# Retention keys and outputs transposed on TensorE into a free PSUM bank, in place of 32x32 block transposes on VectorE

## The chip, the cores and the metric

The kernel runs on one core of one Trainium2 chip. A core has a matrix engine (TensorE, PE in the rows; PEld is its weight load), three elementwise engines (VectorE, DVE; ScalarE, ACT; GpSimd, POOL), a queue that issues transfers (SyncE, SP), an on-chip memory SBUF, and eight accumulator banks of 128 partitions by 512 float32 called PSUM, into which the matrix engine writes. The metric is the device time of one execution in microseconds (us). Each engine works through its own queue in order, and waits where an instruction needs a result of another engine.

## The reference, cut to what matters

Two transformer blocks run one after the other on 1024 tokens of width 1024. The change lies in the second block, in its retention branch with 4 heads, key and value width 256:

```
qb = rotary(split_heads(r_q, 4));  kb = rotary(split_heads(r_k, 4)) * 256 ** -0.5
scores = (q k^T) * gamma^|t-s|  inside a chunk;  intra = scores @ v
step:  out   = (q * q_decay) @ state
       state = state * chunk_decay + (k * k_decay)^T @ v
ret = rms_norm(intra + inter, ret_out_gain);  out_b = merge_heads(ret) * silu(r_g)
```

The state update needs the keys with tokens on the partitions, while the scores need them with features there. The output is normalised with tokens on the partitions and is needed afterwards with features there. So keys and outputs are transposed once each.

## The kernel before

Activations are kept as two float32r parts (a rounded one and the rest), and each product of matrices is three matmuls into one accumulator (`PASSES`). The second block computes stick-breaking attention, then retention, then the merge of both branches. Retention takes the time from about 1440 to 2042 us of the profiled span.

For each head `h` in turn `ret_proj` (L1091) computes the projections: queries and keys with features on the partitions (`dense_col`, L112, copied to `ro` by ACT on L1098), rotated by DVE (L1103 to L1106) and POOL (L1107, L1108); values with tokens on the partitions (`dense_tok`, L102, split into `v` by ACT on L1116 and DVE on L1117); the gate (L1121). The weights are brought in by SP and split by POOL (L70, L71) into `wu`.

`ret_chain` (L1141) then works in two groups `g` of four 128-token tiles `j`. For a group it computes scores (L1151 into `psc`, shown as `pz`), masks and splits them (L1153 to L1157), transposes the keys of the group on DVE with `dve_transpose` (L128) into `kf`, and makes the decayed keys `kd` from `kf`: the rounded part on ACT (L1162), the rest on DVE (L1163). For a tile it computes the output `po` (L1171, L1179; shown as `pt`, in bank "t"), the sum of squares on ACT (L1184), the inverse root on POOL (L125, L126, tile `ss`), the scaled output `ot` on DVE (L1186), and the state update (L1192 into `pst`, shown as `po`, L1196 or L1198, split on L1202 and L1203). After four tiles the group's output is transposed by `dve_transpose` into `ob`, scaled by ACT (L1209), gated by POOL (L1210) and stored by SP (L1212). `kf` and `ob` use one buffer, tag "ob".

`dve_transpose` is 16 instructions, one for each pair of 32-partition blocks:

```
for a in range(4):
    for b in range(4):
        nc.vector.transpose(out=dst[32 * b:32 * b + 32, :, :, 32 * a:32 * a + 32],
                            in_=src[32 * a:32 * a + 32, :, :, 32 * b:32 * b + 32])
```

PSUM is split by tags: three banks "a" for the large products, two "z", and one each of "p", "t" and "o". Retention leaves "p" unused. The order of instructions on each engine is not written out by hand: the framework's scheduler places them by its own estimate of times, and mixes the chain of one head with the projections of the next, and the last chain with the merge products (`merge_logits`, L951). In heads 1 and 2 `attention_gates` (L1125) is mixed in, whose ACT instruction (L1134) waits for a load.

Of the kernel before, what the change touches and what calls it, by code (L numbers as in the profile page):

```python
# [11 lines left out]
F32 = mybir.dt.float32  # L12
F32R = mybir.dt.float32r
AF = mybir.ActivationFunctionType
ALU = mybir.AluOpType
# [4 lines left out]
P = 128  # L20
# [7 lines left out]
def f32(ap):  # L28
    return ap.bitcast(F32)
# [7 lines left out]
def tile_kernel(ctx: ExitStack, tc: tile.TileContext, I: dict, out: bass.AP, dbg=None, stop=None):  # L37
    nc = tc.nc
# [13 lines left out]
    ident = const.tile([P, P], F32, name="ident")  # L52
# [71 lines left out]
    def rsqrt_small(dst, src, mul, eps, eshape):  # L124
        nc.gpsimd.tensor_scalar(out=dst, in0=src, scalar1=mul, scalar2=eps, op0=ALU.mult, op1=ALU.add)  # L125
        nc.gpsimd.tensor_tensor(out=dst, in0=dst, in1=mhalf[:, :eshape], op=ALU.pow)  # L126

    def dve_transpose(dst, src):  # L128

        for a in range(4):  # L130
            for b in range(4):
                nc.vector.transpose(out=dst[32 * b:32 * b + 32, :, :, 32 * a:32 * a + 32],  # L132
                                    in_=src[32 * a:32 * a + 32, :, :, 32 * b:32 * b + 32])

# [944 lines left out]
    with tc.tile_pool(name="rt", bufs=1) as rt:  # L1079
# [61 lines left out]
        def ret_chain(h, tiles):  # L1141
            qTs, kTs, vs = tiles
            state = None
            for g in range(2):
# [3 lines left out]
                for j in range(4):  # L1148
                    cs = slice(j * P, (j + 1) * P)
                    for b in range(2):  # L1150
# [7 lines left out]
                kd = [rt.tile([P, 4, 256], F32R, tag="kd%d" % x, name="kd") for x in range(2)]  # L1158
                kf = rt.tile([P, 4, 256], F32, tag="ob", name="kf")
                dve_transpose(kf.rearrange("p n (b c) -> p b n c", b=2), kT.rearrange("p b (n c) -> p b n c", n=4))  # L1160
                kf, kh, kl = [t_.rearrange("p a b -> p (a b)") for t_ in [kf] + kd]
                nc.scalar.activation(out=kh, in_=kf, func=AF.Copy, scale=rdv[:, h, 0:1])  # L1162
                nc.vector.scalar_tensor_tensor(out=kl, in0=kf, scalar=rdv[:, h, 0:1], in1=f32(kh),  # L1163
                                               op0=ALU.mult, op1=ALU.subtract)
                ot = rt.tile([P, 4, 256], F32, tag="ot", name="ot")
# [38 lines left out]
                ob = rt.tile([P, 2, 4, P], F32, tag="ob", name="ob")  # L1204
                dve_transpose(ob, ot.rearrange("p n (b c) -> p b n c", b=2))
                for b in range(2):
                    ga = rt.tile([P, 512], F32, tag="ga", name="gb", bufs=2)
                    nc.sync.dma_start(out=ga, in_=d_gb[2 * h + b, :, g * 512:(g + 1) * 512])
                    nc.scalar.activation(out=ob[:, b], in_=ob[:, b], func=AF.Copy, scale=rgn[:, 2 * h + b:2 * h + b + 1])  # L1209
                    nc.gpsimd.tensor_tensor(out=ob[:, b].rearrange("p n c -> p (n c)"), in0=ob[:, b].rearrange("p n c -> p (n c)"),  # L1210
# [137 lines left out]
```

## Time and profile before

| | |
|---|---|
| median of 3 runs | 2317.09 us (2314.77 to 2318.42) |
| profiled execution, whole time | 2316.85 us |
| its span on the core | 2315.1 us |
| PE busy | 2182.2 us (94%) |
| DVE busy | 1242.6 us (54%) |
| ACT busy | 879.1 us (38%) |
| POOL busy | 1210.2 us (52%) |

The span reaches from the first instruction to the end of the last; the whole time has 1.75 us more around it. Busy times of engines overlap each other. For PE the busy time holds overlapping matmuls, so the time from the start of one matmul to the start of the next is what a matmul takes of the engine, and the idle time in front of a matmul is what a wait costs.

### The profile page before, as it was taken

The numbers are of one execution on the slowest core, as the hardware profiler recorded it, in microseconds if no ns is written. First come the engines' busy times: TensorE is split into PE (matmuls) and PEld (weight loads), VectorE is DVE, ScalarE is ACT, GpSimd is POOL, SyncE is SP. The second block draws the span as 40 slices with busy tenths as digits, with TensorE's granted clock in tenths as the row PEclk, the third lists the DMA queues.
The fourth block names the chain that finished last, engine by engine and source line by source line (L and its number), as shares of the span: only waits on it lengthen the run. The fifth ranks groups of instructions, "written<-read, shape, count | busy, mean of one in ns | idle before, by whom it ended". The sixth has DMA issues, their size and how long they took to land.

```text
span 2315.1 us, 33643 instructions
## 1 busy us (share of the span) xinstructions
PE 2182.2 (94%) x12197; PEld 1875.5 (81%) x12197; DVE 1242.6 (54%) x2228; ACT 879.1 (38%) x2191; POOL 1210.2 (52%) x1435
## 2 busy tenths in 40 slices
PE   7998888899999988999999999999989999999999
PEld 7777877787898778988888888788878788788887
DVE  4688789844457555665566453327474744321221
ACT  5344434445544225565566544012222222321200
POOL 6667778762004345554565545536575754434531
PEclk9999999999999999999999999999999999999999
DMA  4266830054486431110111103221324333644433
GB/s 129 83 165 166 206 86 26 35 159 130 146 280 215 147 106 42 55 47 23 51 51 55 51 32 97 67 69 55 125 87 132 95 105 101 218 164 152 142 106 107
DMA packets 238791, 249.25 MB, mean 108 GB/s; under 512 B 40032, under 2 KB 173856, under 8 KB 238368
## 3 DMA queue, kind: packets, MB, share of 16 engines
q1 hardware_dynamic: 238624, 247.10, 34.0%
q8 instruction: 96, 1.57, 0.3%
q14 instruction: 71, 0.58, 0.1%
HBM read 171.51 MB, written 75.53 MB: 107 GB/s over the span
## 4 chain that ended last, share of the span: by engine, by line
PE 43%; POOL 7%; DVE 7%; issue 4%; DMA 3%; ACT 3%; SPq 0%; POOLq 0%; ACTq 0%
PE acc L112 26%; PE acc L102 9%; PE acc L859 3%; POOL wu L71 2%; DMA raw<-in_w_in_dram 2%; PE po L1063 2%; DVE A L1042 1%; POOL wu L70 1%; DVE A L1037 1%; POOL A L1047 1%; PE pt L1179 1%; POOL ss L126 1%; ACT A L1036 1%; DVE xo L909 1%; DVE kf L132 1%
## 5 line engine op out<-in xcount | busy, mean ns | idle before, releaser
L112 PE MATMUL acc<-h2h,wu 128*128 128x512 f32 x1504 | 460.5, 396 | 0.7 <-POOL wu L71 0.4
L102 PE MATMUL acc<-wu,h2h 128*128 128x384 f32 (+1 forms) x1536 | 374.5, 326 | 11.5 <-DVE v L1117 5.5
L71 POOL TENSOR_TENSOR wu<-raw,wu 128x512 fp32r<-128x512 f32 (+3 forms) x268 | 364.9, 1370 | 6.1
L70 POOL TENSOR_SCALAR wu<-raw 128x512 fp32r<-128x512 f32 (+3 forms) x268 | 206.3, 773 | 269.1 <-PE acc L112 187.9
L112 PEld LDWEIGHTS acc<-h2h,wu 128*128 128x128 f32 x1504 | 281.8, 188 | 65.2 <-POOL wu L71 0.8
L102 PEld LDWEIGHTS acc<-wu,h2h 128*128 128x128 f32 x1536 | 270.4, 192 | 18.4 <-DVE v L1117 6.3
L112 PE MATMUL acc<-h2l,wu 128*128 128x512 f32 x752 | 277.9, 395 | 0.0
L102 PE MATMUL acc<-wu,h2l 128*128 128x384 f32 (+1 forms) x768 | 248.2, 324 | 0.0
L102 PE MATMUL acc<-wu,h1hi 128*128 128x384 f32 (+2 forms) x768 | 192.2, 334 | 12.7 <-DVE kS L518 6.7
L112 PE MATMUL acc<-h1hi,wu 128*128 128x512 f32 x512 | 164.5, 409 | 7.3 <-ACT pad L315 3.7
L112 PEld LDWEIGHTS acc<-h2l,wu 128*128 128x128 f32 x752 | 141.3, 188 | 31.0
L102 PEld LDWEIGHTS acc<-wu,h1hi 128*128 128x128 f32 x768 | 137.3, 195 | 17.0 <-issue 8.0
L102 PEld LDWEIGHTS acc<-wu,h2l 128*128 128x128 f32 x768 | 147.5, 192 | 1.3
L1047 POOL TENSOR_TENSOR A<-Z,A 128x128 f32<-128x128 f32 (+2 forms) x96 | 111.3, 1165 | 66.3 <-DVE A L1042 48.4
L125 POOL TENSOR_SCALAR ss<-ss 128x2 f32<-128x2 f32 (+2 forms) x136 | 40.7, 300 | 200.4 <-ACT sq L983 144.0
L102 PE MATMUL acc<-wu,h1lo 128*128 128x384 f32 (+2 forms) x384 | 126.8, 333 | 0.0
L112 PEld LDWEIGHTS acc<-h1hi,wu 128*128 128x128 f32 x512 | 98.2, 194 | 32.3 <-ACT pad L315 5.4
L126 POOL TENSOR_TENSOR ss<-ss,mhalf 128x2 f32<-128x2 f32 (+2 forms) x136 | 113.5, 835 | 8.3
L112 PE MATMUL acc<-h1lo,wu 128*128 128x512 f32 x256 | 96.2, 405 | 0.0
L1037 DVE SCALAR_TENSOR_TENSOR A<-Z,A 128x128 f32<-128x128 f32 (+2 forms) x96 | 70.4, 742 | 42.7 <-ACT A L1036 41.8
L1063 PE MATMUL po<-wT,v 128*128 128x512 f32 (+3 forms) x288 | 76.2, 362 | 14.0 <-DVE wT L1061 11.0
L320 DVE SCALAR_TENSOR_TENSOR cv<-pad,c_conv_w,cv 128x1024 f32<-128x1024 f32 x48 | 76.6, 1597 | 1.1
(549 smaller groups left out, 4685.1 us busy)
## 6 DMA issues: line engine op xcount, KB each, us to landing
raw<-in_w_in_dram SPq DMA_DIRECT2D x192, 256.0 KB, 3.0
d_pk<-sct SPq DMA_DIRECT2D x24, 512.0 KB, 4.3
raw<-in_w_out_dram SPq DMA_DIRECT2D x40, 256.0 KB, 2.9
wsa<-d_pk SPq DMA_DIRECT2D x16, 512.0 KB, 6.1
wsb<-d_pk SPq DMA_DIRECT2D x16, 512.0 KB, 7.1
d_sg<-lg SPq DMA_DIRECT2D x32, 256.0 KB, 2.9
sg<-d_sg SPq DMA_DIRECT2D x32, 256.0 KB, 3.4
raw<-in_w_in_dram SPq DMA_DIRECT2D x32, 192.0 KB, 2.7
```

What stands on the lines that cost most here:

```text
L70: nc.gpsimd.tensor_scalar(out=u[:, 0, :], in0=raw, scalar1=1.0, scalar2=0.0, op0=ALU.mult, op1=ALU.add)
L71: nc.gpsimd.tensor_tensor(out=u[:, 1, :], in0=raw, in1=f32(u[:, 0, :]), op=ALU.subtract)
L102: nc.tensor.matmul(acc[:, :n], lhsT=hT[a][:, k, m * P:(m + 1) * P], rhs=us[k][:, b, c0:c0 + n], start=(k == 0 and i == 0), stop=(k == NK - ...
L112: nc.tensor.matmul(accs[half], lhsT=us[k][:, b, c0:c0 + P], rhs=hT[a][:, k, half * 512:(half + 1) * 512], start=(k == 0 and i == 0), stop= ...
L125: nc.gpsimd.tensor_scalar(out=dst, in0=src, scalar1=mul, scalar2=eps, op0=ALU.mult, op1=ALU.add)
L126: nc.gpsimd.tensor_tensor(out=dst, in0=dst, in1=mhalf[:, :eshape], op=ALU.pow)
L132: nc.vector.transpose(out=dst[32 * b:32 * b + 32, :, :, 32 * a:32 * a + 32], in_=src[32 * a:32 * a + 32, :, :, 32 * b:32 * b + 32])
L320: nc.vector.scalar_tensor_tensor(out=cv, in0=pad[:, i:i + T], scalar=conv_w[:, blk, i:i + 1], in1=cv, op0=ALU.mult, op1=ALU.add)
L859: nc.tensor.matmul(acc, lhsT=us[k][:, y, (b % 4) * P:(b % 4 + 1) * P], rhs=token_set(mT[x][:, k, 0:T], s), start=(k == 0 and i == 0), stop ...
L1037: nc.vector.scalar_tensor_tensor(out=A[:, :w], in0=Z[:, :w], scalar=0.0, in1=A[:, :w], op0=ALU.max, op1=ALU.add)
L1047: nc.gpsimd.tensor_tensor(out=A[:, :w], in0=Z[:, :w], in1=A[:, :w], op=ALU.subtract)
L1063: nc.tensor.matmul(po[:, i0 * P:512], lhsT=v[a][:, c0 // P + kb, :], rhs=wT[b][:, :n], start=(diag and kb == 0 and x == 0), stop=(diag == ...
```

## The change

`dve_transpose` goes. The keys of a group are transposed in two halves of two token tiles: four `nc.tensor.transpose` of 128x128 against the identity into bank "p", from which ACT makes the rounded half of `kd` and DVE the rest, reading PSUM; then the same bank takes the second half. The outputs of a group are transposed in two halves `b` of 128 features: four transposes into bank "p", from which ACT makes `ob`, scaled. `kf` goes, and tag "ob" holds `ob` alone.

```
-    def dve_transpose(dst, src):
...
-                kf = rt.tile([P, 4, 256], F32, tag="ob", name="kf")
-                dve_transpose(kf.rearrange("p n (b c) -> p b n c", b=2), kT.rearrange("p b (n c) -> p b n c", n=4))
-                kf, kh, kl = [t_.rearrange("p a b -> p (a b)") for t_ in [kf] + kd]
-                nc.scalar.activation(out=kh, in_=kf, func=AF.Copy, scale=rdv[:, h, 0:1])
-                nc.vector.scalar_tensor_tensor(out=kl, in0=kf, scalar=rdv[:, h, 0:1], in1=f32(kh),
-                                               op0=ALU.mult, op1=ALU.subtract)
+                for x in range(2):
+                    pk = bank("p")
+                    for j in range(2):
+                        for b in range(2):
+                            n = 2 * x + j
+                            nc.tensor.transpose(pk[:, j * 256 + b * P:j * 256 + (b + 1) * P], kT[:, b, n * P:(n + 1) * P], ident)
+                    kh, kl = [t_[:, 2 * x:2 * x + 2, :].rearrange("p a b -> p (a b)") for t_ in kd]
+                    nc.scalar.activation(out=kh, in_=pk, func=AF.Copy, scale=rdv[:, h, 0:1])
+                    nc.vector.scalar_tensor_tensor(out=kl, in0=pk, scalar=rdv[:, h, 0:1], in1=f32(kh),
+                                                   op0=ALU.mult, op1=ALU.subtract)
...
-                dve_transpose(ob, ot.rearrange("p n (b c) -> p b n c", b=2))
                 for b in range(2):
...
-                    nc.scalar.activation(out=ob[:, b], in_=ob[:, b], func=AF.Copy, scale=rgn[:, 2 * h + b:2 * h + b + 1])
+                    pt = bank("p")
+                    for j in range(4):
+                        nc.tensor.transpose(pt[:, j * P:(j + 1) * P], ot[:, j, b * P:(b + 1) * P], ident)
+                    nc.scalar.activation(out=ob[:, b].rearrange("p n c -> p (n c)"), in_=pt, func=AF.Copy, scale=rgn[:, 2 * h + b:2 * h + b + 1])
```

In the changed file the key transposes are on L1157, their ACT and DVE readers on L1159 and L1160, the output transposes on L1207 and their ACT reader on L1208; the other lines of the chain move up by 3 to 7. All engines keep their order up to the first group of head 0, and differ from there.

First place: DVE around the first group of head 0, before. `kf` is the block-transposed keys, `ro` the rotated keys, `wf` the masked scores.

```order
L1105 TENSOR_TENSOR rtmp<-ro,sinT 128x512
L132 STREAM_TRANSPOSE kf<-ro 32x2x4x32 x2
L1106 TENSOR_TENSOR ro<-ro,cosT 128x512
L132 STREAM_TRANSPOSE kf<-ro 32x2x4x32 x14
L1153 TENSOR_TENSOR wf<-pz,rdm 128x512
L1117 TENSOR_TENSOR v<-acc,v 128x256 x3
L1163 SCALAR_TENSOR_TENSOR kd<-kf,rdv,kd 128x1024
L1157 TENSOR_TENSOR wT<-wf,wT 128x512
```

The same place on DVE after the change; `pp` is the bank "p".

```order
L1098 TENSOR_TENSOR rtmp<-ro,sinT 128x512
L1099 TENSOR_TENSOR ro<-ro,cosT 128x512
L1146 TENSOR_TENSOR wf<-pz,rdm 128x512
L1160 SCALAR_TENSOR_TENSOR kd<-pp,rdv,kd 128x512
L1150 TENSOR_TENSOR wT<-wf,wT 128x512
L1110 TENSOR_TENSOR v<-acc,v 128x256 x3
L1160 SCALAR_TENSOR_TENSOR kd<-pp,rdv,kd 128x512
```

The 16 transposes that stood between the rotation and the values' split are gone, and the one `kd` of 1024 columns has become two of 512, one of them ahead of the values' split.

Second place: DVE around the second group of head 0, before.

```order
L132 STREAM_TRANSPOSE ob<-ot 32x8x32 x16
L1103 TENSOR_TENSOR rtmp<-ro,cosT 128x512
L1104 TENSOR_TENSOR rtmp<-ro,sinT 128x512
L1105 TENSOR_TENSOR rtmp<-ro,sinT 128x512
L1106 TENSOR_TENSOR ro<-ro,cosT 128x512
L1103 TENSOR_TENSOR rtmp<-ro,cosT 128x512
L132 STREAM_TRANSPOSE kf<-ro 32x2x4x32 x16
L1186 TENSOR_SCALAR ot<-pt,rdv,ss 128x256
L1105 TENSOR_TENSOR rtmp<-ro,sinT 128x512
L1163 SCALAR_TENSOR_TENSOR kd<-kf,rdv,kd 128x1024
```

The same place on DVE after the change.

```order
L1096 TENSOR_TENSOR rtmp<-ro,cosT 128x512
L1097 TENSOR_TENSOR rtmp<-ro,sinT 128x512
L1098 TENSOR_TENSOR rtmp<-ro,sinT 128x512
L1099 TENSOR_TENSOR ro<-ro,cosT 128x512
L1096 TENSOR_TENSOR rtmp<-ro,cosT 128x512
L1098 TENSOR_TENSOR rtmp<-ro,sinT 128x512
L1183 TENSOR_SCALAR ot<-pt,rdv,ss 128x256
L1160 SCALAR_TENSOR_TENSOR kd<-pp,rdv,kd 128x512
L1195 SCALAR_TENSOR_TENSOR st<-st,rdv,po 128x512
L1160 SCALAR_TENSOR_TENSOR kd<-pp,rdv,kd 128x512
L1200 TENSOR_TENSOR ss__15532<-st,ss__15531 128x512
```

The two blocks of 16 are gone; the second half of `kd` now stands between the state `st` and its split `ss_`.

Third place: PE in the second group of head 0, before, at the first state update.

```order
L102 MATMUL acc<-wu,h2h 128x256 x2
L1171 MATMUL pt<-v,wT 128x256 x3
L1192 MATMUL po<-v,kd 128x256 x2
L102 MATMUL acc<-wu,h2l 128x256
L102 MATMUL acc<-wu,h2h 128x256 x2
L102 MATMUL acc<-wu,h2l 128x256
L102 MATMUL acc<-wu,h2h 128x256
L1192 MATMUL po<-v,kd 128x256 x4
```

The same state update on PE after the change; the first four key transposes of the group stand 22 matmuls ahead of its first row here.

```order
L112 MATMUL acc<-h2l,wu 128x512
L1189 MATMUL po<-v,kd 128x256 x2
L112 MATMUL acc<-h2h,wu 128x512 x2
L1157 MATMUL pp<-ident,ro 128x128 x4
L1189 MATMUL po<-v,kd 128x256 x4
L112 MATMUL acc<-h2h,wu 128x512 x2
```

The second four key transposes now stand inside the first state update, behind its first two matmuls.

## Rows read from the trace of the kernel before

**Rows 1.** Page part 1: busy us, share of the span and instructions, by engine
```profile
PE 2182.2 (94%) x12197; PEld 1875.5 (81%) x12197; DVE 1242.6 (54%) x2228; ACT 879.1 (38%) x2191; POOL 1210.2 (52%) x1435
```

**Rows 2.** Stretches: start:end, length, busy us (instructions) by engine, PEclk, DMA share, GB/s
```profile
1480.00:1520.00 40.00, 34.26 (x240) 31.86 (x239) 21.45 (x33) 5.30 (x11) 22.27 (x20) 0.96 0.18 53
...
1600.00:1640.00 40.00, 39.05 (x279) 37.50 (x280) 28.40 (x43) 10.12 (x26) 22.83 (x23) 0.91 0.13 39
...
1680.00:1720.00 40.00, 37.96 (x186) 31.59 (x185) 27.84 (x49) 11.22 (x24) 25.14 (x25) 0.97 0.23 70
```

**Rows 3.** Waits of PE, 1440 to 2042 us: waiter, releaser, us in total, times, longest
```profile
PE acc L102 <- DVE v L1117: 5.5, 4, 3.2
PE pt L1171 <- DVE ot L1186: 4.3, 4, 2.0
PE pz L1151 <- POOL ro L1108: 3.4, 4, 1.2
PE po L1192 <- ACT kd L1162: 3.2, 3, 2.0
PE acc L102 <- POOL wu L71: 2.7, 5, 0.9
PE po L1192 <- DVE kd L1163: 2.2, 3, 1.0
PE pt L1179 <- DVE ss__16598 L1203: 1.6, 1, 1.6
PE po L1192 <- DVE st L1198: 1.0, 2, 0.6
```

**Rows 4.** Groups of DVE instructions, 1440 to 2042 us: busy us, mean ns, idle before
```profile
L132 DVE STREAM_TRANSPOSE ob<-ot 32x256 f32<-32x256 f32 x128 | 55.8, 436 | 1.9
L132 DVE STREAM_TRANSPOSE kf<-ro 32x256 f32<-32x256 f32 x128 | 55.8, 436 | 24.6 <-DMA d_ob<-ob 23.0
```

**Rows 5.** Timeline of DVE: start us, us, instructions, idle before in brackets
```profile
1499.05 6.29 DVE L132 STREAM_TRANSPOSE kf<-ro 32x256 f32<-32x256 f32 x14
...
1592.18 7.17 DVE L132 STREAM_TRANSPOSE kf<-ro 32x256 f32<-32x256 f32 x16
...
1709.68 7.19 DVE L132 STREAM_TRANSPOSE kf<-ro 32x256 f32<-32x256 f32 x16 [1.47 <-DMA d_ob<-ob]
```

**Rows 6.** Timeline of PE: three waits, and one row without a wait
```profile
1506.44 0.80 PE L102 MATMUL acc<-wu,h2h 128*128 128x256 f32 x2 [3.19 <-DVE v L1117]
...
1544.41 0.52 PE L1171 MATMUL pt<-v,wT 128*128 128x256 f32 x3
...
1599.98 0.62 PE L1171 MATMUL pt<-v,wT 128*128 128x256 f32 x3 [1.96 <-DVE ot L1186]
...
1733.26 1.83 PE L1151 MATMUL pz<-ro 128*128 128x128 f32 x14 [1.18 <-POOL ro L1108]
```

**Rows 7.** Timeline of PE around eight 128x128 transposes of the attention branch (L1058)
```profile
1429.32 0.60 PE L1058 MATMUL pt<-ident,A 128*128 128x128 f32 x4
1429.75 0.60 PE L1058 MATMUL pp<-ident,A 128*128 128x128 f32 x4
1430.11 0.47 PE L112 MATMUL acc<-h2h,wu 128*128 128x512 f32 x1
1430.42 0.39 PE L112 MATMUL acc<-h2l,wu 128*128 128x512 f32 x1
1430.65 0.63 PE L112 MATMUL acc<-h2h,wu 128*128 128x512 f32 x2
```

**Rows 8.** Single lines: duration ns min/median/max, first and last start, form
```profile
L1058 PE MATMUL pt<-ident,A x160: 270/272/435, 901.2 to 1429.6; 128*128 128x128 f32 x160
L1162 ACT ACTIVATE kd<-kf,rdv x8: 1148/1150/1154, 1505.4 to 1947.2; 128x1024 fp32r<-128x1024 f32 x8
L1198 DVE SCALAR_TENSOR_TENSOR st<-st,rdv,po x24: 730/740/751, 1551.8 to 1963.5; 128x512 f32<-128x512 f32 x24
```

**Rows 9.** Waits of ACT, 1480 to 2000 us: waiter, releaser, us in total, times, longest
```profile
ACT ga L1134 <- DMA ga<-d_ga: 34.9, 10, 5.9
```

More of the change, by code (lines that the diff above doesn't have):

```diff
@@ L126, in rsqrt_small @@
         nc.gpsimd.tensor_tensor(out=dst, in0=dst, in1=mhalf[:, :eshape], op=ALU.pow)
-    def dve_transpose(dst, src):
[L130 to L133, printed above, removed]
     class Halves:
```

## The prediction

> **What bounds the kernel now.** I read the page's busy times first: PE is busy 94% of the span, the others about half [rows 1]. A change that moves work on to PE must therefore pay for itself in PE's own time. Next I cut the retention stretch (1440 to 2042 us) into pieces of 40 us. There PE falls to 34.3 of 40 where the chains are dense, and its granted clock to 0.96, 0.91 and 0.97 [rows 2]. Third, I read what PE waits for there [rows 3]: the eight largest releasers make 23.7 us, spread over DVE, ACT's and DVE's `kd`, and POOL. Fourth, the DVE groups: 256 block transposes of 436 ns, 2 x 55.8 = 111.6 us, in blocks of 16 that hold DVE for 7.2 us at a time; in front of them DVE stood 23.0 us more, since `kf` wants the buffer of `ob`, which a store still reads [rows 4, 5]. DVE works in order, so whatever stands behind a block comes 7 us or more later. The timeline shows it: a block runs from 1499.05 for 6.29 us, and PE waits 3.19 us for the values' split behind it; a block ends at 1599.35, and PE waits 1.96 us for the `ot` right behind it [rows 5, 6]. So the stretch is bound by PE, with some 24 us of gaps, a good part made by these blocks.
>
> **The change part by part.**
>
> *Transposes on PE.* 8 groups x (8 key + 8 output) = 128 transposes; the order lists 128 PE instructions more and no block transpose on DVE. Their price is the step, not the length of one row. Between 1429.32 and 1430.42 lie eight fp32 transposes of the same size and one matmul of 512 columns, whose step is 1430.65 - 1430.42 = 0.23 us: (1.10 - 0.23) / 8 = 0.109 us [rows 7]. 128 x 0.109 = **+14.0 us**. PE has no slack except its waits, so all of it counts; if a fifth falls into waits that remain, it is 11 us.
>
> *DVE's blocks go.* What PE gets back is counted wait by wait [rows 3]. `kd` follows `kf` directly: 3.2 + 2.2 = 5.4 us, all of it. Of the values' split the longest, 3.2 us, stood behind a block; the other three stay. Of `ot` the longest, 2.0; the others wait for POOL's root. State and its split, 1.6 + 1.0 = 2.6, lie in the jam of DVE work within 20 us of a block such as the one at 1709.68 [rows 5]. Of the rotated keys from POOL (3.4 in four) two of up to 1.2, one at 1733.26 in the same jam [rows 6]: 2.4. Sum **-15.6 us**. In the order (first place) nothing stands between the rotation and `wf` any more, and in the second place `ot` comes one rotation step after the last, instead of behind 16 transposes. What is late next is POOL: its weight split (2.7) and its share of `ot`, which nothing here moves.
>
> *The clock.* In three pieces it was granted at 1.2 instead of 2.4 GHz for a while: 40 x (0.04 + 0.09 + 0.03) = 6.4 us lost [rows 2]. The first two pieces hold the 3.19 us wait and, just ahead of the second's left edge, the 1.96 us wait [rows 6]; their falls I take as gone, 40 x 0.13 = **-5.2 us**; the third I leave.
>
> *Restarts.* The three matmuls behind the 1.96 us wait take 0.62 us against 0.52 without a wait [rows 6]. Some 15 waits x 0.1 = **-1.5 us**.
>
> *Readers of the bank.* ACT made `kd` in 1.15 us for 1024 columns; now two halves, about 0.6 each. DVE's half reads PSUM; the nearest form is the state update, 0.74 us for 512 columns [rows 8]. Output scaling on ACT changes only its source. None is on the path: ACT and DVE have idle half the stretch. POOL and SP keep their instructions. SP's store of `ob` no longer holds DVE.
>
> *New waits.* The bank is one, and is filled four times in a group. Behind the first four key transposes the second four wait for ACT's and DVE's half, 0.6 + 0.74 = 1.3 us and queueing, and behind them on PE's queue stand the state matmuls and all products. In the third place 27 matmuls, 22 of them of 512 columns (5 us at 0.23), lie between; in the first place 15 of 256 columns, about half as long each, some 1.8 us, are the thinnest cover. For the outputs, the transposes wait for the same `ot` as the next tile's bank "t" does, so no new one, except the second half, with 18 or more matmuls ahead. No row shows this wait. From below it is 0 (all covered); a gain is excluded, since no such wait exists now. From above I take what PE loses to `kd` today for one hand-over in a group, 5.4 us, twice: 10.8. I take **+2.0**, nearer to the lower end because the covers exceed the 1.3 us.
>
> Sum: 14.0 - 15.6 - 5.2 - 1.5 + 2.0 = -6.3 us. From the profiled execution's 2316.85 us (span 2315.1 and 1.75 around it; 0.24 below the median of 2317.09): **2310.5 us**, -0.27%.
>
> **A rule against it.** Eight transposes in 0.87 us of PE time is what the rows show [rows 7]. The Trainium skill, "VectorE: DVE Perf Modes", section "The three transpose paths", lists 390 ns for a 128x128 bf16 transpose on TensorE against 311 on VectorE; by it the first term would be 128 x 0.39 = 50 us (an estimate from that page), and the kernel clearly slower. The trace does not agree for transposes in a row.
>
> **The rivals.**
>
> *One bank, filled late (slower).* ACT works in order, and in heads 1 and 2 its gate instruction stands waiting for a load 10 times, 3.5 us each, up to 5.9 [rows 9]. Where it stands ahead of a reader of bank "p", the next fill stalls on PE, and all products behind it. Covers are about 2 to 5 us. If half of the 32 fills stall 1.0 us each, that is 16 us in place of the 2.0: 2310.5 + 14.0 = 2324.5. It is slower than before once the new waits come to over 8.3 us (6.3 + 2.0), 0.5 us on each of those 16 fills. Against it: ACT is idle most of the stretch, and only two heads have that load. The Trainium skill, "Perfetto Trace Analysis", section "Matmuls", says that independent groups should rotate through different PSUM banks so that emptying one overlaps filling the next; keeping to one bank goes against that, and no run here shows it yet for bank "p".
>
> *The waits move (no change).* DVE's blocks go, but PE then waits at the same places for POOL, which is busy 52% with the weights' split and the roots. If half of the waits and of the clock come back: 14.0 - 7.8 - 2.6 - 0.8 + 2.0 = +4.8, cut to about +2 by transposes that fall into these waits: 2319. For it: `ot` waits on POOL today. Against: `kd`, the largest, has no POOL in it.
>
> *Transposes do not overlap (slower).* A row of one transpose is 272 ns [rows 8]; if each took that of PE, 34.8 us, the time is 2331. Against it: [rows 7].
>
> *All gaps close (faster).* All 23.7 us of waits and all 6.4 of the clock: 14.0 - 23.7 - 6.4 - 2.0 = -18.1: 2298.7. Against it: POOL's part does not change.
>
> That the change does not do what it says is excluded by the order.
>
> **How the numbers follow.** Forecast 0.57, with its own span 2302 to 2316 (0.45 of it faster by over 0.2%, 0.12 within); one bank 0.12; the waits move 0.19; no overlap 0.02; all gaps close 0.10. 0.2% is 4.6 us, about what a measurement of this kernel can tell from no change. Faster: 0.45 + 0.10 = 0.55. Within: 0.12 and 0.15 of the moved waits, 0.27. Slower: the moved waits' other 0.04, one bank's 0.12 and 0.02: 0.18. The range for 8 in 10 leaves out half of "all gaps close" below and most of the slow cases above: 2300 to 2322.
>
> **What would show it.** Right: no transpose row on DVE, DVE's busy time some 112 us less; 128 PE rows on bank "p" whose steps are 0.11 us; PE's waits for `kd`, for the values at the first group and for state gone; the clock 1.00 where it was 0.96 and 0.91; the stretch shorter by about 6 us, and all before and behind it as it was. Wrong: waits of PE on ACT or DVE readers of "p" above 5 us in all (one bank); larger waits on POOL (moved); steps of 0.2 or more at full clock; or a clock that falls in new places.

## The result and the profile after

The changed kernel takes 2304.38 us (median of 5 runs, 2301.96 to 2306.7) against 2317.09: a ratio of 0.9947, 95% interval 0.9934 to 0.9961. That is 12.7 us less; the forecast was 6.3 less. Its profiled execution has a span of 2300.2 us and is the fastest of the five, so the two profiled executions lie 14.9 us apart in span, a little more than the medians. Here is part 1 of its page, as in [rows 1]:

```profile
PE 2188.1 (95%) x12325; PEld 1885.9 (82%) x12325; DVE 1126.4 (49%) x1980; ACT 881.8 (38%) x2199; POOL 1195.8 (52%) x1435
```

PE has 128 instructions more and DVE 116 us less work. The stretches of [rows 2] in the changed kernel, and one behind them:

```profile
1480.00:1520.00 40.00, 38.39 (x273) 35.69 (x273) 14.62 (x18) 5.82 (x13) 22.76 (x20) 1.00 0.18 54
1600.00:1640.00 40.00, 39.29 (x263) 35.85 (x261) 10.67 (x18) 8.96 (x22) 19.12 (x20) 1.00 0.27 88
1680.00:1720.00 40.00, 37.58 (x226) 32.62 (x225) 22.99 (x23) 11.70 (x25) 33.28 (x30) 1.00 0.34 111
...
1700.00:1740.00 40.00, 36.67 (x278) 35.05 (x277) 21.43 (x29) 11.94 (x28) 31.88 (x32) 0.96 0.41 133
```

PEclk (the value behind the five engines) is 1.00 where it was 0.96 and 0.91. The third fall, which began at 1717.6 us before, now begins at 1720.9 and is still there. PE's waits in retention, as in [rows 3] (waiter, releaser, us in total, times, longest; 1440 to 2028 us):

```profile
PE po L1189 <- DVE st L1195: 2.9, 2, 1.7
PE acc L102 <- POOL wu L71: 1.4, 1, 1.4
PE acc L102 <- DVE v L1110: 1.3, 3, 0.7
PE pz L1144 <- POOL ro L1100: 0.9, 1, 0.9
PE pz L1144 <- POOL ro L1101: 0.7, 1, 0.7
PE acc L112 <- ACT lg L949: 0.4, 1, 0.4
PE po L1189 <- ACT kd L1159: 0.2, 1, 0.2
```

The rows add up to 7.8 us; before, all such rows of the stretch came to 26.0. The wait for `ot` is gone, `kd` has 0.2 us left, and no row has a transpose (`pp`) waiting for the bank. The timeline of DVE at the first group of head 0 (start, us, instruction) shows how, against the first line of [rows 5]:

```profile
1497.36 0.68 DVE L1146 TENSOR_TENSOR wf<-pz,rdm 128x512 f32<-128x512 f32 x1
1497.96 0.73 DVE L1160 SCALAR_TENSOR_TENSOR kd<-pp,rdv,kd 128x512 fp32r<-128x512 f32 x1
1498.72 1.64 DVE L1150 TENSOR_TENSOR wT<-wf,wT 128x512 fp32r<-128x512 f32 x1
1500.28 1.07 DVE L1110 TENSOR_TENSOR v<-acc,v 128x256 fp32r<-128x256 f32 x3
```

And the timeline of PE at the same point, where [rows 6] has 3.19 us of waiting:

```profile
1500.75 0.50 PE L102 MATMUL acc<-wu,h2h 128*128 128x256 f32 x2 [0.26 <-DVE v L1110]
```

The new lines one by one (duration ns min/median/max, first and last start, form), beside [rows 8]:

```profile
L1157 PE MATMUL pp<-ident,ro x64: 270/272/274, 1494.0 to 1931.1; 128*128 128x128 f32 x64
...
L1159 ACT ACTIVATE kd<-pp,rdv x16: 670/689/692, 1496.2 to 1931.5; 128x512 fp32r<-128x512 f32 x16
...
L1160 DVE SCALAR_TENSOR_TENSOR kd<-pp,rdv,kd x16: 735/746/753, 1498.0 to 1932.6; 128x512 fp32r<-128x512 f32 x16
```

So a half of `kd` costs 0.69 + 0.75 us, beside the 0.6 + 0.74 of the working.

**A measure for what follows.** In the kernels below the time from the start to the first retention scores varies between 1493.8 and 1504.6 us, although the work ahead of it is the same (in the last two, where it is not, 1495.6 and 1506.3). One total is therefore a blunt measure. Beside it I use the retention stretch in the profiled execution: from the first score matmul (`pz`) to the first product of the merge (`acc<-oah`). It is 548.5 us before and 534.1 after; behind it all kernels take 272.3 to 273.2 us. From the starts of PE's instructions I split the stretch (with the 12 us ahead of it) into PE's own steps at full clock (0.232 us for 512 columns, 0.119 for 256, 0.112 for 128), its idle gaps by releaser, half of the time that the clock was granted at 1.2 GHz, and the rest. Everything beyond PE's own steps is called the excess. Two limits: each row is one execution, and how far the stretch varies between executions of one kernel is not measured, so differences of a few us between rows are no finding by themselves; and half-clock time in which PE stood idle is counted under idle as well as under clock (0.9 us too much in the clock column before, 3.3 in ballast_keys), which makes the rest too small by as much.

| kernel | ratio to before, 95% interval | stretch | excess | idle | of it for DVE / POOL / ACT | clock | rest |
|---|---|---|---|---|---|---|---|
| before | 1 | 548.5 | 41.9 | 26.2 | 15.1 / 7.6 / 3.6 | 6.8 | 8.9 |
| after | 0.9947 [0.9934, 0.9961] | 534.1 | 13.2 | 8.0 | 4.2 / 3.0 / 0.7 | 1.7 | 3.5 |
| twice | 1.0008 [0.9991, 1.0025] | 548.1 | 12.8 | 7.5 | 5.0 / 2.0 / 0.4 | 1.7 | 3.7 |
| two_banks | 0.9952 [0.9927, 0.9977] | 537.0 | 16.1 | 9.2 | 6.7 / 2.5 / 0 | 3.4 | 3.4 |
| keys_on_pe | 1.0017 [1.0005, 1.0028] | 550.0 | 36.2 | 23.1 | 6.7 / 15.2 / 1.3 | 5.1 | 8.0 |
| outs_on_pe | 0.9970 [0.9959, 0.9982] | 538.5 | 24.7 | 14.0 | 10.1 / 3.0 / 0.8 | 3.4 | 7.3 |
| kf_own_buffer | 1.0097 [1.0081, 1.0112] | 570.0 | 63.4 | 41.7 | 20.1 / 19.7 / 1.9 | 15.4 | 6.4 |
| ballast | 1.0024 [1.0012, 1.0036] | 550.9 | 30.0 | 18.5 | 9.2 / 7.9 / 1.4 | 6.8 | 4.7 |
| ballast_keys | 1.0097 [1.0076, 1.0117] | 566.4 | 45.5 | 31.2 | 21.4 / 8.8 / 1.0 | 11.9 | 2.3 |
| ballast_outs | 0.9955 [0.9938, 0.9972] | 536.6 | 15.6 | 9.9 | 2.0 / 5.6 / 2.3 | 1.7 | 4.0 |
| no_transposes | 0.9957 [0.9946, 0.9968] | 537.3 | 30.7 | 18.9 | 5.0 / 11.1 / 2.8 | 8.5 | 3.3 |
| no_key_blocks | 1.0012 [0.9999, 1.0026] | 552.5 | 45.9 | 23.6 | 5.3 / 14.7 / 3.7 | 17.1 | 5.2 |
| keys_pe_gates_first | 1.0026 [1.0008, 1.0043] | 546.0 | 37.5 | 20.7 | 6.9 / 13.0 / 0.8 | 11.9 | 4.9 |
| after_gates_first | 0.9998 [0.9982, 1.0014] | 543.1 | 27.1 | 18.1 | 5.3 / 11.1 / 1.7 | 3.4 | 5.6 |

Every one of these kernels has its own order of instructions from head 0 on (the two with the gates first from about 1459 us), since the scheduler places the work anew for each. That turned out to matter.

### The profile page after: what moved, and what is told of

The parts are those of the page before. It is cut to its first block, busy times and chain, and to the rows that moved or that the text cites. A ratio compares the mean times of both kernels' runs of the same rounds, so it can differ in the third digit from the quotient of the medians.

```text
span 2300.2 us, 33638 instructions
## 1 busy us (share of the span) xinstructions
PE 2188.1 (95%) x12325; PEld 1885.9 (82%) x12325; DVE 1126.4 (49%) x1980; ACT 881.8 (38%) x2199; POOL 1195.8 (52%) x1435
## 4 chain that ended last, share of the span: by engine, by line
PE 57%; DVE 14%; POOL 10%; issue 7%; DMA 5%; ACT 4%; SPq 1%; POOLq 0%; DVEq 0%; ACTq 0%
PE acc L112 28%; PE acc L102 12%; PE acc L852 3%; POOL wu L71 2%; POOL wu L70 2%; DMA raw<-in_w_in_dram 2%; DVE X L458 2%; DVE svt L456 2%; PE po L1056 1%; DVE A L1035 1%; DVE cv L313 1%; POOL ss L126 1%; DVE A L1030 1%; PE pz L545 1%; POOL A L1040 1%
## 5 line engine op out<-in xcount | busy, mean ns | idle before, releaser
L71 POOL TENSOR_TENSOR wu<-raw,wu 128x512 fp32r<-128x512 f32 (+3 forms) x268 | 359.2, 1349 | 5.8
L70 POOL TENSOR_SCALAR wu<-raw 128x512 fp32r<-128x512 f32 (+3 forms) x268 | 201.5, 756 | 273.2 <-PE acc L112 190.5
L102 PEld LDWEIGHTS acc<-wu,h2h 128*128 128x128 f32 x1536 | 266.8, 190 | 11.9 <-PE pp L1051 3.3
```

The source lines that it names most:

```text
L70: nc.gpsimd.tensor_scalar(out=u[:, 0, :], in0=raw, scalar1=1.0, scalar2=0.0, op0=ALU.mult, op1=ALU.add)
L71: nc.gpsimd.tensor_tensor(out=u[:, 1, :], in0=raw, in1=f32(u[:, 0, :]), op=ALU.subtract)
L102: nc.tensor.matmul(acc[:, :n], lhsT=hT[a][:, k, m * P:(m + 1) * P], rhs=us[k][:, b, c0:c0 + n], start=(k == 0 and i == 0), stop=(k == NK - ...
```

## The experiments

An edit is shown against the changed kernel, except where a run is said to start from another one.

### What a transpose costs on PE, and whether one bank holds it up

**twice**: the changed kernel with each transpose issued twice into the same columns.

```
-                            nc.tensor.transpose(pk[:, ...], kT[:, b, n * P:(n + 1) * P], ident)
+                            for _ in range(2):
+                                nc.tensor.transpose(pk[:, ...], kT[:, b, n * P:(n + 1) * P], ident)
```

> The changed kernel with each of TensorE's transposes issued twice into the same place, 128 more. If all of TensorE's time in the stretch counts: 128 x 0.110 = +14.1 us, the stretch 548, the kernel 2318. If such transposes fall into waits: +8 or less. If a second fill of the one bank were held by its readers, it would be more than 14, since the bank is held longer.

The stretch grew from 534.1 to 548.1, 14.0 us for 128 more transposes or 0.109 us each, and the ratio by 0.0061, 14.1 us of 2317. The idle time stayed (8.0 and 7.5 us). The groups of the transposes in PE's view (busy us, mean ns, idle before):

```profile
L1209 PE MATMUL pp<-ident,ot 128*128 128x128 f32 x128 | 20.6, 272 | 0.0
L1158 PE MATMUL pp<-ident,ro 128*128 128x128 f32 x128 | 16.7, 272 | 0.0
```

256 transposes, each 272 ns long, and PE never idle before one. The price is the step, and with the excess as small as here it all counts: the first of the three cases expected.

**two_banks**: the second half of each pair goes to a "z" bank.

```
-                    pk = bank("p")
+                    pk = bank("pz"[x])
...
-                    pt = bank("p")
+                    pt = bank("pz"[b])
```

> The changed kernel with the second half of the keys and of the outputs in a bank z instead of p. If the one bank holds TensorE: what it still waits for ACT's and VectorE's readers goes, and the stretch falls from 534.1 to some 530. If the covers suffice, as the profile says (0.2 us of waits for kd, none for p): 534 within 2.

The ratio is that of the changed kernel (0.9952 and 0.9947), the stretch 2.9 us longer, with waits for `v` and `ot` that have nothing to do with the bank. For the changed kernel the rival that one bank is filled late falls (in other orders of the same work the bank did hold PE up, as the gates-first runs below show). It falls although what it feared came to pass: ACT stood longer at the gates' loads than in [rows 9]. ACT's wait in the changed kernel, 1480 to 2000 us:

```profile
ACT ga L1127 <- DMA ga<-d_ga: 50.1, 16, 5.5
```

### One half of the change

**keys_on_pe** takes the keys' half alone; the outputs stay block transposes on DVE.

```
                 ob = rt.tile([P, 2, 4, P], F32, tag="ob", name="ob")
+                dve_transpose(ob, ot.rearrange("p n (b c) -> p b n c", b=2))
                 for b in range(2):
...
-                    pt = bank("p")
-                    for j in range(4):
-                        nc.tensor.transpose(pt[:, j * P:(j + 1) * P], ot[:, j, b * P:(b + 1) * P], ident)
-                    nc.scalar.activation(out=ob[:, b].rearrange("p n c -> p (n c)"), in_=pt, ...)
+                    nc.scalar.activation(out=ob[:, b], in_=ob[:, b], ...)
```

> Only the keys are transposed on TensorE; the outputs stay as block transposes on VectorE. PE gets 64 transposes more, 64 x 0.110 = +7.0 us. Theory A (the key blocks make the waits: they stand on VectorE ahead of kd, the values' split and ot, while nothing on PE waits for what stands behind an output block): the whole gain at half the price, 18.3 us of waits, 5.1 of the clock, 5.1 of restarts go, so 2317 + 7 - 28 = 2296, faster than the changed kernel. Theory B (what counts is how busy VectorE is, each kind of block half): half the gain of the full change, 2311. Theory C (the gain is the luck of another order of instructions): anything within 7 us of 2311 without a pattern.

**outs_on_pe** takes the outputs' half alone; the keys stay as before.

```
-                for x in range(2):
-                    pk = bank("p")
...
+                kf = rt.tile([P, 4, 256], F32, tag="ob", name="kf")
+                dve_transpose(kf.rearrange("p n (b c) -> p b n c", b=2), kT.rearrange("p b (n c) -> p b n c", n=4))
```

> Only the outputs are transposed on TensorE; the keys stay as block transposes on VectorE, in the buffer they share with the outputs. PE gets 64 transposes more, +7.0 us. Theory A: PE's waits for kd, values and ot stay (some 24 us), so 2317 + 7 = 2322 to 2324. Theory B: half the gain, 2311. Theory C: no pattern.

The keys' half gains nothing (1.0017), the outputs' half 7 us (0.9970). That is the reverse of what the forecast's terms said, which gave `kd` and `v`, 8.6 us, to the key blocks. In keys_on_pe the waits for DVE did fall, from 15.1 to 6.7 us; but those for POOL rose from 7.6 to 15.2. The two halves' changes do not add up to the whole. Of the theories set down, A misses both kernels, and B (2311) meets only the second (2311.82); the first, at 2323.5, is also outside the 7 us that C allowed.

### Blocks on DVE as a load

If what matters is that the blocks occupy DVE, then blocks whose result nobody reads should bring the waits back. **ballast** adds both kinds to the changed kernel, into a buffer of their own; **ballast_keys** only the first, **ballast_outs** only the second.

```
+                kf = rt.tile([P, 4, 256], F32, tag="kf", name="kf")
+                dve_transpose(kf.rearrange("p n (b c) -> p b n c", b=2), kT.rearrange("p b (n c) -> p b n c", n=4))
                 for x in range(2):
                     pk = bank("p")
...
+                od = rt.tile([P, 2, 4, P], F32, tag="kf", name="kf")
+                dve_transpose(od, ot.rearrange("p n (b c) -> p b n c", b=2))
```

> The changed kernel, and besides it all 256 block transposes on VectorE into a buffer that nobody reads, at their old places in the code: VectorE is as busy as before, but kd and the outputs don't depend on the blocks. If VectorE's occupation makes the waits: those other than for kd come back (18.3 - 5.4 = 13 us, 5 of the clock, 3 of restarts), 2318 to 2326, slower than before, since the 14.1 us of TensorE's transposes stay. If it was the path from kf to kd and the held buffer: 2304 to 2309.

> The changed kernel with the 128 key block transposes alone added on VectorE, into a buffer that nobody reads. The stretch from the first score product of retention to the first product of the merge took 534.1 us in the changed kernel and 550.9 with all 256. If what counts is how long VectorE is held: half of 16.8, 542 to 543. If it is what stands behind a block: the kernel with key blocks alone lost 11 us beyond PE's own work more than the changed one, and the one with output blocks alone 23, so 537 to 541 here.

> The changed kernel with the 128 output block transposes alone added on VectorE, into a buffer that nobody reads. If what counts is how long VectorE is held: the same stretch takes 542 to 543 us. If it is what stands behind a block: the output blocks stand in one row of 16 behind the last ot of a group, in front of the next head's rotation, and cost the more, 546 to 552.

With all blocks back, ballast came out at 2324.97, inside the 2318 to 2326 expected if occupation makes the waits, and the waits for DVE, for POOL and the clock all rose again (4.2 to 9.2, 3.0 to 7.9, 1.7 to 6.8 us). But the kinds do not add up: the key blocks alone cost 32 us of stretch, the output blocks alone 2.5, and both together 17, less than the key blocks alone. Both expectations for the parts (542 to 543 us of stretch for each, or 537 to 541 and 546 to 552) miss the measured 566.4 and 536.6. Divided by eight groups, the same 7.2 us of an in-order engine cost 0.3 us in one kernel and 4 us in another. PE's waits in ballast_keys (the two largest):

```profile
PE acc L102 <- DVE v L1117: 12.3, 5, 5.7
PE pz L1151 <- POOL ro L1107: 5.3, 4, 3.4
```

and in ballast_outs (the three largest):

```profile
PE acc L102 <- POOL wu L71: 4.4, 4, 1.8
PE pt L1183 <- ACT ss__17693 L1206: 1.8, 1, 1.8
PE acc L102 <- DVE v L1117: 1.7, 3, 1.0
```

Key blocks read `ro`, so they become ready in the midst of the rotation; the 12.3 us show them ahead of the values' split. Output blocks read the last `ot` of a group, and PE waited little for what followed them on DVE here. That the place of a block decides is a reading of these rows; no run moves a block and nothing else.

**kf_own_buffer** starts from the kernel before, with the one difference that `kf` has a buffer of its own, so that DVE does not stand for the store of `ob` (23.0 us, [rows 4]).

```
-                kf = rt.tile([P, 4, 256], F32, tag="ob", name="kf")
+                kf = rt.tile([P, 4, 256], F32, tag="kf", name="kf")
```

> The kernel before, with one edit: kf gets a buffer of its own, so that the key blocks need not wait for the store of the last outputs, which held VectorE 23.0 us in six places. If this hold is what makes the key blocks late: PE's waits for kd (5.4 us) and for state and values behind them fall by about half, 2306 to 2311. If the 7.2 us of a block alone make them: 2314 to 2318, with the hold gone and the waits as before.

It is 21.5 us of stretch slower. DVE's timeline shows where the blocks went once nothing held them:

```profile
1872.35 7.17 DVE L132 STREAM_TRANSPOSE kf<-ro 32x256 f32<-32x256 f32 x16
...
1883.41 5.81 DVE L132 STREAM_TRANSPOSE kf<-ro 32x256 f32<-32x256 f32 x13
1889.23 7.18 DVE L132 STREAM_TRANSPOSE ob<-ot 32x256 f32<-32x256 f32 x16
1896.44 0.42 DVE L1117 TENSOR_TENSOR v<-acc,v 128x256 fp32r<-128x256 f32 x1
```

PE at the same time:

```profile
1896.92 0.58 PE L102 MATMUL acc<-wu,h2h 128*128 128x256 f32 x1 [5.25 <-DVE v L1117]
```

A split of 0.42 us stood behind 13 us of blocks, and PE waited 5.25 us for it. POOL's share of the waits rose too, from 7.6 to 19.7. So the 23.0 us in which DVE stood in the kernel before can't be counted as a loss of that size: they went (1.8 us of idle time are left ahead of the key blocks), and the kernel got slower, where 2306 to 2318 had been expected. What the hold alone cost is not shown, since the order changed with it.

### Work left out

**no_key_blocks** starts from the kernel before and leaves out its key blocks: `kd` is made from the rotated keys as they are, so the keys are not transposed at all.

```
-                kf = rt.tile([P, 4, 256], F32, tag="ob", name="kf")
-                dve_transpose(kf.rearrange("p n (b c) -> p b n c", b=2), kT.rearrange("p b (n c) -> p b n c", n=4))
-                kf, kh, kl = [t_.rearrange("p a b -> p (a b)") for t_ in [kf] + kd]
+                kf, kh, kl = [t_.rearrange("p a b -> p (a b)") for t_ in [kT] + kd]
```

> The kernel before with only its key blocks left out: the decayed keys are made straight from the rotated keys (another result), the output blocks stay on DVE and are read. No PE transposes. Theory A (the key blocks make the waits): excess of the retention stretch falls from 41.9 to about that of the unread output blocks, 16, and the time to about 2291. Rival (output blocks that are read cost as much, as the kernel with keys alone on PE suggests with its excess of 36.2): excess about 36 with POOL's waits of about 15, time about 2311.

56 us of work are gone and nothing was added, and yet the stretch is not shorter: 4.0 us longer in the profiled execution, and the ratio of 1.0012 has 1 at the edge of its interval. My expectation of 2291 us falls; of the rival's, the waits for POOL came (14.7 of about 15), the time of 2311 did not. PE's waits behind 1570 us (the two largest):

```profile
PE acc L102 <- POOL wu L71: 11.4, 10, 2.6
PE acc L102 <- DVE v L1117: 3.6, 3, 1.8
```

The waits for DVE fell from 15.1 to 5.3, but PE now waits for the weights' split on POOL. POOL's timeline ahead of one such wait (idle time before, and what ended it, in brackets):

```profile
1710.69 1.49 POOL L1135 TENSOR_TENSOR oa<-oa,ga 128x512 f32<-128x512 f32 x1 [3.10 <-DMA oa<-d_oa]
...
1717.63 1.29 POOL L1135 TENSOR_TENSOR oa<-oa,ga 128x512 f32<-128x512 f32 x1 [2.47 <-DMA oa<-d_oa]
1718.89 1.06 POOL L70 TENSOR_SCALAR wu<-raw 128x512 fp32r<-128x512 f32 x1
1719.92 1.69 POOL L71 TENSOR_TENSOR wu<-raw,wu 128x512 fp32r<-128x512 f32 x1
```

The matmul on PE that needed this split:

```profile
1721.66 0.39 PE L102 MATMUL acc<-wu,h2h 128*128 128x256 f32 x1 [1.74 <-POOL wu L71]
```

POOL stood 3.10 and 2.47 us for loads of `oa`, the attention's output, which it multiplies by the gates; the split of weights was queued behind the second. With a wait comes the clock; the stretch from 1720 us:

```profile
1720.00:1760.00 40.00, 34.33 (x241) 32.80 (x242) 25.68 (x39) 8.17 (x19) 30.75 (x29) 0.87 0.38 115
```

PEclk is 0.87, and over the whole stretch the half clock costs 17.1 us, against 6.8 before.

**no_transposes** is the changed kernel with both transposes left out: `kd` from the rotated keys and `ob` from the outputs as they are.

```
-                    pk = bank("p")
-                    for j in range(2): ...
+                    pk = kT[:, x, :]
...
-                    pt = bank("p")
-                    for j in range(4): ...
-                    nc.scalar.activation(out=ob[:, b].rearrange("p n c -> p (n c)"), in_=pt, ...)
+                    pt = ot[:, :, b * P:(b + 1) * P]
+                    nc.scalar.activation(out=ob[:, b], in_=pt, ...)
```

> The changed kernel with both transposes left out: the decayed keys are made straight from the rotated keys and the outputs are scaled untransposed, so no engine transposes anything (the result is therefore another one). ACT, DVE and POOL do what they do after the change. If PE's 128 transposes cost their 0.110 us each and nothing else, as the kernel with each transpose twice showed, the time is that of after less 14.1: about 2290.3, and the retention stretch about 520 us with an excess over PE's own steps of about 13, as after. If bank p or its readers also cost something, the excess is smaller than after's 13.2, by what they cost. If the schedule's placement moves the sum by chance, the excess differs either way by several us with no wait that names the cause.

PE has 14.3 us less to do than after the change, and yet the stretch is 3.2 us longer in the profiled execution and the ratio (0.9957) no better; 2290 us had been expected if the transposes cost their steps and nothing else moved. Again it is POOL: 11.1 us of waits, and 8.5 us of half clock. POOL's group of the gates (busy us, mean ns, idle before and what ended it) in this kernel:

```profile
L1128 POOL TENSOR_TENSOR oa<-oa,ga 128x512 f32<-128x512 f32 x16 | 21.4, 1337 | 48.0 <-DMA oa<-d_oa 40.9 <-ACT ga L1127 7.0
```

The same group in the changed kernel:

```profile
L1128 POOL TENSOR_TENSOR oa<-oa,ga 128x512 f32<-128x512 f32 x16 | 21.6, 1347 | 29.5 <-ACT ga L1127 26.2 <-DMA oa<-d_oa 2.2 <-ACT gv L1114 1.1
```

This idle time sorts all fourteen kernels. Where POOL stands over 40 us ahead of the gates (keys_on_pe 43.2, kf_own_buffer 40.1, no_transposes 48.0, no_key_blocks 43.5, the two with the gates first 55.0 and 53.4), PE waits 11.1 to 19.7 us for POOL. Where it stands 25.7 to 36.3 us (the other eight), PE waits 2.0 to 8.8 us for it. Inside the eight the two do not go together: 25.7 us stand beside 7.6 before, 36.3 beside 2.5 in two_banks.

### The gates first

To test that, the attention gates were issued ahead of the first head instead of inside heads 1 and 2, once in keys_on_pe (**keys_pe_gates_first**) and once in the changed kernel (**after_gates_first**).

```
-                    if h in (1, 2):
-                        take(ag, 1)
...
+        take(ag, 16)
         for h in range(4):
             ret_chain(h, ret_proj(h))
```

> Keys on PE, output blocks on DVE (the kernel that took 2323.5), with the attention gates, which POOL multiplies after a load in heads 1 and 2, moved ahead of the first head. Theory P (in that kernel POOL stands waiting for the gate's loads, 31.6 us in 8 waits, and PE waits for POOL's weight split, rotation and root behind them): PE's waits for POOL fall from 15 to about 3, and the time to about 2311, if the gates' work ahead of the stretch costs nothing. Rival (the waits come from the output blocks' place on DVE, or from the schedule's placement without one cause): PE's waits for POOL stay at 10 or more, time above 2318.

> The changed kernel with the attention gates ahead of the first head, as the control of the run beside it and as an attempt at a faster kernel. Theory P: PE's waits for POOL are only 3.0 after the change, so at most these and 0 to 3 us are won: 2301 to 2305. Rival (placement without one cause): 2304 plus or minus 6, with new waits.

The edit moved the gates to 1447 to 1569 us, beside the projections and the first chains, and there they met the same jam: POOL's idle time ahead of them rose to 55.0 and 53.4 us. So the test does not show the gates' work gone, only elsewhere. What can be read is the part behind 1570 us, which no longer has gates. PE's waits there in keys_on_pe, gates in place (first rows):

```profile
PE acc L102 <- POOL wu L71: 5.8, 6, 2.1
PE pt L1175 <- DVE ot L1190: 4.6, 3, 3.0
PE pz L1151 <- POOL ro L1107: 4.1, 2, 3.1
PE pz L1151 <- POOL ro L1108: 2.6, 3, 1.2
```

and in keys_pe_gates_first (all rows):

```profile
PE pp L1164 <- DVE kd L1167: 5.3, 1, 5.3
PE acc L102 <- POOL wu L71: 4.3, 3, 1.9
PE pz L1151 <- POOL ro L1108: 1.2, 2, 0.8
PE pz L1151 <- POOL ro L1107: 1.2, 1, 1.2
```

POOL's share fell from 13.6 (with 1.1 in smaller rows) to 6.7 us, not to 3, and a new wait of 5.3 us took much of it back. That one is the wait the prediction had named: the second fill of bank "p" (`pp`) held up by a reader of the first. DVE's timeline there:

```profile
1746.23 7.17 DVE L132 STREAM_TRANSPOSE ob<-ot 32x256 f32<-32x256 f32 x16
1753.43 0.75 DVE L1167 SCALAR_TENSOR_TENSOR kd<-pp,rdv,kd 128x512 fp32r<-128x512 f32 x1
```

and PE's:

```profile
1754.24 1.11 PE L1164 MATMUL pp<-ident,ro 128*128 128x128 f32 x4 [5.29 <-DVE kd L1167]
```

A block of outputs stood ahead of the 0.75 us that would have emptied the bank. Such rows, none in the changed kernel, come to 6.9 us here over the whole stretch, 3.0 in ballast, 2.1 in ballast_keys, 1.2 in after_gates_first and 0.5 in keys_on_pe. So one bank is enough in the changed kernel's order, and not in general. The total did not fall (2325.6, not 2311), and PE's waits for POOL came to 13.0 over the stretch (15.2 in keys_on_pe): by the numbers set down the theory of the gates fails and its rival holds, though the waits went where the gates went. after_gates_first says the same from the other side: behind 1570 us its waits come to 6.3 us, as after the change (6.1), and the additional ones (18.1 us in all, against 8.0) lie ahead of it, where the gates now stand. It is no faster kernel (2320.1, where either theory allowed 2310 at most).

So that POOL standing at the gates holds back the weights' split is shown at one place by the timelines above, and goes with the waits over fourteen kernels in two groups. That it is the whole cause of POOL's waits is not shown. Giving `oa` a second buffer, so that its load starts earlier, would test it; that was not tried.

## Why the prediction was right, and where its sizes were off

The time came out 12.7 us below before, within the range (2300 to 2322) and on the likeliest side; the stretch shrank by 14.4 us and nothing else did. Term by term, in the stretch of the profiled executions:

| step | forecast | measured | how |
|---|---|---|---|
| 128 transposes on PE | +14.0 | +14.3 | own steps 518.6 to 532.9; twice: 0.109 each |
| `kd` | -5.4 | -5.2 | 5.4 to 0.2 |
| values' split | -3.2 | -4.2 | 5.5 to 1.3 |
| `ot` | -2.0 | -4.3 | 4.3 to 0 |
| state and its split | -2.6 | -0.1 | 3.0 to 2.9 |
| rotated keys from POOL | -2.4 | -2.7 | 4.3 to 1.6 |
| weights' split on POOL | 0 | -1.7 | 3.1 to 1.4 |
| new waits for bank "p" | +2.0 | 0 | no row has one |
| clock | -5.2 | -5.1 | 6.8 to 1.7 |
| restarts | -1.5 | -5.4 | rest 8.9 to 3.5 |
| sum | -6.3 | -14.4 | |

**Transposes.** Right in size and in reason: the step, not the row's length, and no slack to hide it. The price of 390 ns that the prediction quoted from the Trainium skill, "VectorE: DVE Perf Modes", section "The three transpose paths", is not what a transpose takes of PE in a row: twice shows 0.109 us.

**The mis-sized terms.** Two make nearly the whole difference of 8 us. First, the waits: 18.2 us went, net 13.6 had been forecast. `ot` was read as waiting for POOL's root except for one place; without blocks all of it went. State's wait stayed, so the jam near 1710 was not made by the blocks alone. That the waits for state would be gone, one of the signs set down, did not come true. And the new waits, for which a lower end of 0 had been given, were 0: the covers of 15 to 27 matmuls did exceed the 0.69 + 0.75 us. That needed readers with nothing long ahead of them; where the order put more ahead, the wait appeared (6.9 us in keys_pe_gates_first). Second, the restarts. Only the row behind a wait had been read, at 0.1 us. The matmul ahead of a wait loses too: it is followed by nothing, so its full 0.28 us counts where in a row only the step of 0.12 would. Counting idle gaps over 0.15 us, there were 31 before and 10 after, and these tails come to 5.0 and 1.6 us, 0.16 for each wait. They make 3.4 of the 5.4 us by which the rest fell; the other 2.0 are what was called restarts, 0.1 for each of 21 waits, not 15. That split is an estimate: the rest is a remainder, and over the fourteen kernels it runs from 0.10 to 0.41 us for each wait. Two sums of the prediction are slightly off: its eight largest rows of waits add up to 23.9, not 23.7, and all rows to 26.0, which "all gaps close" should have used (about 2296.5 in place of 2298.7).

**The rivals.** One bank filled late: excluded for the changed kernel by two_banks and by the missing rows; in five of the other kernels the bank did hold PE up, by 0.5 to 6.9 us, most where blocks on DVE (not ACT's gate, as the rival had it) stood ahead of a reader. No overlap: excluded by twice. All gaps close gave 2298.7, a little nearer to the median than the forecast (5.7 against 6.1 us off), but 7.8 us of waits and one fall of the clock remain. The waits move to POOL is the one that deserved more: in the changed kernel it did not happen (POOL's share fell from 7.6 to 3.0), but in keys_on_pe, no_key_blocks and no_transposes it did, with 11.1 to 15.2 us.

**What this means for the gain.** The forecast took the order around the blocks as given and subtracted their waits one by one. The runs show that this holds for the kernel as it was scheduled, and not in general: taking out the key blocks and adding nothing did not shorten the stretch (552.5 against 548.5), and neither did taking PE's transposes out of the changed kernel (537.3 against 534.1). Each edit makes the scheduler place the gates, splits and rotations anew, and the placement can be worth up to 14 us here (excess 13.2 after, 16.1 with two banks, 27.1 with the gates first, with the same transposes and elementwise work, ratios 0.9947, 0.9952 and 0.9998). So the price of 14 us and the loss of DVE's waits are shown; how much of the 12.7 us, twice what was forecast, is owed to a favourable placement of POOL's work is not settled; what is owed to it, the forecast did not foresee, and that part is luck. With POOL's waits and the clock as in no_transposes (8.1 and 6.8 us more) the result would, by this estimate, have been about no change, so the sign, too, rests in part on that placement.

## What to carry to other kernels

Where a scheduler sets the order, a removed instruction frees its engine but also re-deals the order of all the others; look up what the next engine in line (here POOL, with gates that wait for loads ahead of the weights' split) has queued in order, and give the case in which it becomes the bound a real chance. A wait on a busy TensorE costs more than its idle time: the matmul ahead of it that runs out alone, the one behind it that starts alone, and the clock. A long block on an in-order engine is priced by what stands behind it: the same 7 us cost 0.3 us in one kernel here and 4 in another. And a single accumulator bank that is refilled needs its readers early in their engines' queues.

## What the runs showed of the hardware

- 128x128 float32 transposes in a row take 0.109 us of PE each, though a row is 272 ns; repeating all of them added 14.0 us to the stretch and no idle time (8.0 and 7.5 us).
- The granted clock (2.4 GHz, or 1.2 where it fell) came down at waits of PE, and the longest wait was not always the one. Before, a fall began at 1506.0 us, inside the longest wait (3.19 us, up to 1506.44). In the changed kernel the one fall in the stretch began at 1720.9 us, behind three shorter waits, while a single longer one, of 1.73 us, brought none:

```profile
1715.96 0.98 PE L1189 MATMUL po<-v,kd 128*128 128x256 f32 x6 [1.14 <-DVE st L1195]
...
1719.36 0.49 PE L1144 MATMUL pz<-ro 128*128 128x128 f32 x2 [0.90 <-POOL ro L1100]
...
1720.58 3.12 PE L1144 MATMUL pz<-ro 128*128 128x128 f32 x14 [0.73 <-POOL ro L1101]
...
1831.39 0.97 PE L1189 MATMUL po<-v,kd 128*128 128x256 f32 x6 [1.73 <-DVE st L1195]
```

- In no_key_blocks the clock read 0.87 over 40 us, and half clock cost 17.1 us in its stretch, beside 23.6 us of waits.
- ACT stood 50.1 us at the gates' loads in the changed kernel, against 34.9 before, and PE waited only 0.6 us for ACT in the stretch. It was not without effect: 26.2 us of POOL's idle time ahead of the gates ended with ACT's gate instruction.
